# Expert rows fetched in two halves of 4 KB, and 24 sample slots ahead of the fence

## The chip, the cores and the metric

The kernel runs on one core of a Trainium2 chip. The metric is the device time of one execution, in microseconds. Three executions of the kernel before took 1599.02, 1606.98 and 1607.16 us. The core has five engines that work side by side and wait for one another by semaphores: PE (TensorE), DVE (VectorE), ACT (ScalarE), POOL (GpSimd) and SP (SyncE, which here only issues loads and stores). Sixteen DMA engines move the data between memory and the core for all of them.

## The reference

One decoder layer for 512 prompt tokens and 32 sample tokens (8 sequences of 4), all in float32. Retention heads and a convolution branch are mixed, added to the input and normalised; then every token goes through an expert layer, and is normalised again. The change lies in the expert layer:

```python
q = (xb @ w_query).reshape(PEER_BLOCK, PEER_HEADS, PEER_DQ)      # 8 heads
v1, i1 = lax.top_k(s1, PEER_TOPK)                                # 16 of 128 keys, twice
sv, ci = lax.top_k(cand, PEER_TOPK)                              # 16 of the 256 pairs
idx = e1 * N_KEYS + e2                                           # one of 16384 experts
gate = jax.nn.softmax(sv.astype(jnp.float32), axis=-1)
u = jnp.take(peer_u, idx, axis=0)
act = jax.nn.gelu(jnp.einsum('phkd,pd->phk', u, xb), approximate=False)
vv = jnp.take(peer_v, idx, axis=0)
return jnp.einsum('phk,phkd->pd', gate * act, vv)
```

Each token thus needs 8 x 16 = 128 experts, and each expert is a row u and a row v of 1024 numbers (4 KB each).

## The kernel before

The host puts u and v of an expert side by side in one row of 8 KB (the array uv) and lays out a second copy of u for matmuls (ut).

**Two ways through the expert layer.** The last 256 prompt tokens take the dense way: all 16384 experts are computed by matmuls, 128 keys at a time. A scoring stage (`scores_of`, L778) loads 0.5 MB of ut and makes 16 matmuls (L784); its result goes through a gelu on ACT. `build` (L855) makes the tokens' weights for each key from one-hot matrices (ACT L862 and L864, DVE L866 and L870, PE L875); `first_keys` (L888) multiplies them into the arrays Gb, Ga and Gc (DVE L899 and L901), `last_keys` (L907) makes Gd. A v stage (`v_stage`, L914) loads 0.5 MB of v rows and adds 8 matmuls to the sums in PSUM (L920). There are 128 scoring stages and 128 v stages; both take their loads from a pool of four buffers (`uvp`, L759), by SP's queue.

**The fetched way.** The other tokens, the first 256 of the prompt and the 32 samples, fetch only the experts that they need (`gather`, L567). A slot is one indirect transfer that POOL issues (L572): for each of 128 partitions the row of 8 KB that the index names, 1 MB in all. Then DVE multiplies the u half with the token and sums it (the dot, L575), ACT makes the gelu and multiplies it by the gate (L579, L580), and DVE adds v times that weight to the sum (the update, L585). Group 0 (`gather0`, tokens 0 to 127) has 128 slots, the samples s have 32 (each token on four partitions, with two heads on each), group b (tokens 128 to 255) has 128: 288 slots. The buffers are three in the pool `gp` (L99), and a fourth for every fourth slot, `gx` for the first 60 slots of group 0 and `gx2` for group b, which is opened behind the fence (L964). So samples that are fetched ahead of the fence have three buffers.

**Order of the work.** The program is written group by group, and a scheduler puts the instructions of each engine into one fixed order that it finds by its own estimate of the times. What the author adds are order constraints: the last instruction of `first_keys` is the fence (L963), and `gather` puts the dots of group b, and those of the samples from slot `FREE` on, behind it on DVE (L576, L577). `FREE` is 12 (L36): 12 sample slots may run ahead of the fence, 20 behind it. Behind the fence `run` (L597, L965) writes down the v stages, `last_keys` and the remaining 32 scoring stages (`phases`, L923), in turn with the rest of the slots (`fetched`, L944).

**What each step waits for.** A slot's transfer waits for the update that last read its buffer. The dot waits for the whole transfer. The update waits for ACT. The instructions of one engine run in their order, so a dot whose rows are late holds up everything behind it on DVE. The first multiply L899 frees the PSUM bank that the next matmuls of `build` write (two banks, `pdn`, L761). At the end, `finish` (L588) normalises the last group, and the two blocks of the dense way are normalised and stored (L966 to L971).

The indices come out of the top-k as floats; a cast on DVE writes them as integers into I0, Is and Ib (L685, L795).

Of the kernel before, what the change touches and what calls it, by code (L numbers as in the profile page):

```python
# [15 lines left out]
OP = mybir.AluOpType  # L16
# [3 lines left out]
D = 1024  # L20
# [12 lines left out]
TB = 8  # L33
KX = 60
UV = 4
FREE = 12  # L36
EG = (32, 20, 44, 32)
E0S = (0, 32, 52, 96)

# [54 lines left out]
def tile_step(ctx: ExitStack, tc: tile.TileContext, a, o):  # L94
    nc = tc.nc
    V, S, T, G = nc.vector, nc.scalar, nc.tensor, nc.gpsimd
# [17 lines left out]
    def mmps():  # L114
        turn[0] += 1
        return banks[turn[0] % len(banks)].tile([128, 512], F32, name="mm")
# [17 lines left out]
    def load_w(view, c0, places=(), after=None):  # L134

        ws = []
        for q in range(2):
            w = wp.tile([128, 8, 256], F32, name="w") if not places or places[q] is None else places[q]
            load = nc.sync.dma_start(w, view[c0 // 256 + q])
            if after is not None:  # L140
                behind(load, after)
            ws.append(w)
        return ws
# [21 lines left out]
    def behind(ins, other):  # L165
        tc.add_manual_dep(ins.ins, other.ins.name, mybir.DependencyInfo(
            mybir.DependencyClass.NoSync, mybir.DependencyReason.DATA), reason="order")

    def small(name, shape, dt=F32, bufs=2):
        return wk.tile(shape, dt, name=name, bufs=bufs)  # L170
# [24 lines left out]
    def project(w, m, xT, c0, n):  # L195
        p = mmps()
        for k in range(8):
            T.matmul(p[:, :n], w[m // 2][:, k, (m % 2) * 128:(m % 2 + 1) * 128], xT[:, k, c0:c0 + n],  # L198
                     start=(k == 0), stop=(k == 7))
        return p[:, :n]  # L200
# [366 lines left out]
    def gather(x1, idx, gate, acc, slots):  # L567

        for k in slots:
            spare = gx if x1 is x1_0 and k < KX else (gx2[0] if gx2 and len(slots) == 128 else None)  # L570
            t = (spare if spare is not None and k % 4 == 3 else gp).tile([128, 2 * D], F32, name="g")
            G.indirect_dma_start(out=t, out_offset=None, in_=a["uv"],  # L572
                                 in_offset=bass.IndirectOffsetOnAxis(ap=idx[:, k:k + 1], axis=0))
            act = gw.tile([128, 2], F32, name="act")
            dot = V.scalar_tensor_tensor(t[:, :D], t[:, :D], 1.0, x1, op0=OP.mult, op1=OP.mult, accum_out=act[:, 0:1])  # L575
            if fence and (len(slots) == 128 or k >= FREE):  # L576
                behind(dot, fence[0])  # L577
            wgt = gw.tile([128, 1], F32, name="wgt")
            S.activation(act[:, 1:2], act[:, 0:1], AF.Gelu)  # L579
            S.activation(wgt, act[:, 1:2], AF.Copy, scale=gate[:, k:k + 1])  # L580
            v = t[:, D:]
            if k == slots[0]:
                S.activation(acc, v, AF.Copy, scale=wgt)
            else:
                V.scalar_tensor_tensor(acc, v, wgt, acc, op0=OP.mult, op1=OP.add)  # L585
            yield
# [22 lines left out]
    E0 = per.tile([128, PH, TK], F32, name="E0")  # L609
    GT0 = per.tile([128, PH, TK], F32, name="GT0")  # L610
    I0 = per.tile([128, PH * TK], I32, name="I0")
    acc0 = per.tile([128, D], F32, name="acc")
    GSP = {"s": (32, 4), "b": (128, 1)}
    Eg, GTg, Ig = {}, {}, {}
# [46 lines left out]
    for q in range(2):  # L661
        c = slice(q * 512, (q + 1) * 512)
# [12 lines left out]
    for h0 in range(0, PH, 2):  # L675
        w = load_w(a["w_query"], h0 * 256)
        qq = small("qe", [128, 4, 128], bufs=1)
        for hs in ([h0], [h0 + 1]) if h0 == 0 else ([h0, h0 + 1],):
            for h in hs:
                for s in range(2):  # L680
                    m = (h - h0) * 2 + s
                    S.activation(qq[:, m], project(w, m, x1T0, 0, 128), AF.Copy)
            retrieve(lambda h, s: qq[:, (h - h0) * 2 + s], hs, 128, 1, E0, GT0, hs[0], led and (lambda ins: behind(ins, led[0])))
            ss = slice(hs[0] * TK, (hs[-1] + 1) * TK)
            c = V.tensor_copy(I0[:, ss], E0.rearrange("p h k -> p (h k)")[:, ss])  # L685
            led = led or [c]
    conv_s(yS)
    retain_s(qS, kS, vs[0], gS, last0)
# [2 lines left out]
    r = slice(NS, n)  # L691
# [98 lines left out]
    def topk_of(g, c0, which):  # L790
        w_, r_ = GSP[g]
        for h0 in which:
            retrieve(lambda h, s: qs[:, h * 2 + s, c0:c0 + w_], [h0] if r_ > 1 else [h0, h0 + 1], w_, r_, Eg[g], GTg[g], h0)
            ss = slice(h0 * TK, (h0 + (1 if r_ > 1 else 2)) * TK)
            V.tensor_copy(Ig[g][:, ss], Eg[g].rearrange("p h k -> p (h k)")[:, ss])  # L795

    for h0 in range(0, PH, 2):
        w = load_w(a["w_query"], h0 * 256)
# [6 lines left out]
    for g in range(2):  # L805
# [9 lines left out]
        p = mmps().rearrange("p (q t) -> p q t", q=4)  # L815
# [7 lines left out]
        for q in range(3):  # L823
            V.tensor_copy(gtT[:, q, cs], gr)
            if q < 2:
                V.tensor_sub(gr, gr, gtT[:, q, cs])
    topk_of("b", NS, range(0, PH, 2))
    topk_of("s", 0, range(2))
    for e in range(E0S[2], E0S[3]):
        S.activation(place(e), scores_of(e), AF.Gelu)  # L830
# [135 lines left out]
    for b in range(2):  # L966
        t = uvp.tile([128, D], F32, name="uv")
        layer_norm(t, 128, ln2[0], ln2[1], pB[b])
        for q in range(2):
            c = slice(q * 512, (q + 1) * 512)  # L970
# [47 lines left out]
```

## Time and profile before

| what | us |
|---|---|
| runs shown | 1599.02, 1606.98, 1607.16 |
| profiled execution | 1603.19 |
| its span, first to last instruction | 1601.4 |
| PE, DVE, ACT, POOL busy | 1494.5, 1225.3, 604.3, 374.1 |
| first slot of group 0 issued | 129.7 |
| sample slots issued, first and last | 776.5, 1065.3 |
| slots of group b issued, first and last | 992.6, 1567.4 |

The profile is of one execution. Busy times of engines overlap. In the windows, columns are: stretch and its length, busy us (and count) of PE, PEld (PE's weight loads), DVE, ACT and POOL, then the granted clock of PE, the mean busy share of the 16 DMA engines, and GB/s; asked for one line, only its engines have columns. In the timeline a row is start, duration, engine, line and operation, and in brackets how long the engine was idle ahead of it and what ended that. A line of the chain of waits is start, duration and what ran. In the table of transfers a row has minimum, median and maximum in ns, and the first and last start. The matmuls' ends are modelled, so the distance of starts says more than the busy share.

### The profile page before, as it was taken

How to read it: one execution, taken by the hardware profiler on the slowest of the kernel's cores; microseconds unless marked ns; L12 is line 12 of the kernel's file. 1: busy time of each engine (PE TensorE's matmuls, PEld its weight loads, DVE VectorE, ACT ScalarE, POOL GpSimd, SP SyncE). 2: the span in 40 equal slices, each digit the busy share in tenths (PEclk: the TensorE clock that was granted, in tenths of full speed). 3: DMA queues.
4: the chain of work that ended last, by engine and by line, in shares of the span. 5: the costliest groups of instructions: out<-in, count | busy, mean ns of one | idle time of the engine just before them, and what ended most of it. 6: DMA issues, size and time to landing. Idle time of an engine off the chain costs nothing.

```text
span 1601.4 us, 20802 instructions
## 1 busy us (share of the span) xinstructions
PE 1494.5 (93%) x7014; PEld 1010.1 (63%) x7014; DVE 1225.3 (77%) x3158; ACT 604.3 (38%) x1687; POOL 374.1 (23%) x335
## 2 busy tenths in 40 slices
PE   6899999996979999999999997999999999999996
PEld 6788556564756667788788875444566655543332
DVE  3939989989865999999852788566777777766666
ACT  2235542254222323333623888413994111111111
POOL 1001423444321222321120000122223222222221
PEclk9899999998989999999999997999999999999998
DMA  9458778997698669997794321998999999999995
GB/s 355 180 195 347 253 280 301 354 364 253 253 383 321 260 250 340 345 340 271 251 413 157 108 86 57 398 402 332 385 365 380 423 424 424 424 423 424 424 424 211
DMA packets 99543, 503.75 MB, mean 315 GB/s; under 512 B 10183, under 2 KB 21191, under 8 KB 56549
## 3 DMA queue, kind: packets, MB, share of 16 engines
q0 software_dynamic: 42240, 305.12, 48.7%
q1 hardware_dynamic: 50749, 189.96, 31.3%
q10 hardware_dynamic: 6448, 7.36, 1.5%
q8 instruction: 55, 0.90, 0.2%
q14 instruction: 51, 0.42, 0.1%
HBM read 497.03 MB, written 5.80 MB: 314 GB/s over the span
## 4 chain that ended last, share of the span: by engine, by line
PE 32%; DMA 28%; DVE 24%; issue 8%; ACT 4%; POOL 2%; SPq 0%; DVEq 0%; POOLq 0%; ACTq 0%
DMA g<-in_uv_dram,Ib 17%; PE pB L920 10%; PE sp L784 9%; PE mm L198 7%; DMA g<-in_uv_dram,I 7%; DVE acc L585 6%; DVE g L575 4%; POOL g L572 2%; ACT off L862 2%; PE mm L875 2%; PE mm L308 2%; DMA g<-in_w_in_dram 2%; DMA uv<-in_uv_dram 1%; DVE iu L504 1%; DVE score L505 1%
## 5 line engine op out<-in xcount | busy, mean ns | idle before, releaser
L784 PE MATMUL sp<-x1T,uv 128*128 128x256 f32 x2048 | 464.7, 384 | 15.4 <-ACT Ga L830 9.4
L784 PEld LDWEIGHTS sp<-x1T,uv 128*128 128x128 f32 x2048 | 385.5, 191 | 89.5 <-issue 23.2
L585 DVE SCALAR_TENSOR_TENSOR acc<-g,wgt,acc 128x1024 f32<-128x1024 f32 x285 | 365.0, 1281 | 99.3 <-ACT wgt L580 98.1
L572 POOL DMA_INDIRECT g<-in_uv_dram,I x128 | 181.9, 1421 | 435.1 <-DVE acc L585 222.6
L579 ACT ACTIVATE act<-act 128x1 f32<-128x1 f32 x288 | 57.9, 201 | 592.4 <-DVE g L575 592.0
L575 DVE SCALAR_TENSOR_TENSOR g<-g,x1g 128x1024 f32<-128x1024 f32 x160 | 195.3, 1224 | 94.2 <-DMA g<-in_uv_dram,Ib 63.1
L572 POOL DMA_INDIRECT g<-in_uv_dram,Ib x128 | 133.5, 1043 | 517.9 <-DVE acc L585 318.5
L575 DVE SCALAR_TENSOR_TENSOR g<-g,x 128x1024 f32<-128x1024 f32 x128 | 155.6, 1217 | 31.9 <-DMA g<-in_uv_dram,I 31.8
L198 PE MATMUL mm<-x1T,w 128*128 128x384 f32 (+1 forms) x512 | 176.1, 500 | 0.2 <-ACT score L524 0.2
L920 PE MATMUL pB<-uv,Ga 128*128 128x512 f32 x352 | 162.1, 604 | 1.1 <-DMA uv<-in_uv_dram 0.8
L862 ACT ACTIVATE off<-row,e1T 128x128 bf16<-128x128 bf16 x512 | 157.8, 388 | 1.5 <-PE mm L875 0.4
L198 PEld LDWEIGHTS mm<-x1T,w 128*128 128x128 f32 x512 | 96.6, 190 | 71.4 <-issue 37.9
L920 PE MATMUL pB<-uv,Gd 128*128 128x512 f32 x256 | 117.2, 601 | 2.1 <-DMA uv<-in_uv_dram 1.0
L920 PE MATMUL pB<-uv,Gb 128*128 128x512 f32 x256 | 115.4, 604 | 2.9 <-DMA uv<-in_uv_dram 2.5
L920 PEld LDWEIGHTS pB<-uv,Ga 128*128 128x128 f32 x352 | 63.7, 189 | 83.7 <-issue 63.1
L920 PEld LDWEIGHTS pB<-uv,Gd 128*128 128x128 f32 x256 | 46.1, 189 | 73.3 <-issue 48.2
L875 PEld LDWEIGHTS <-A 128*128 128x128 bf16 x1536 | 64.6, 100 | 36.6 <-issue 32.0
L920 PEld LDWEIGHTS pB<-uv,Gb 128*128 128x128 f32 x256 | 48.1, 193 | 59.6 <-issue 54.3
L875 PE MATMUL mm<-B,A 128*128 128x96 bf16 (+1 forms) x1536 | 68.4, 197 | 13.3 <-DVE Gc L901 12.4
L864 ACT ACTIVATE A<-off 128x1024 bf16<-128x1024 bf16 x64 | 67.4, 1053 | 28.1 <-PE mm L875 27.7
L870 DVE TENSOR_TENSOR B<-M,gtT 128x768 bf16<-128x768 bf16 (+1 forms) x192 | 69.8, 419 | 9.8 <-PE mm L875 9.6
L920 PE MATMUL pB<-uv,Gc 128*128 128x512 f32 x160 | 72.3, 599 | 0.0
(279 smaller groups left out, 1706.3 us busy)
## 6 DMA issues: line engine op xcount, KB each, us to landing
uv<-in_ut_dram SPq DMA_DIRECT2D x128, 512.0 KB
uv<-in_uv_dram SPq DMA_DIRECT2D x128, 512.0 KB
w<-in_w_in_dram SPq DMA_DIRECT2D x18, 1024.0 KB
w<-in_w_query_dram SPq DMA_DIRECT2D x16, 1024.0 KB
w<-in_w_out_dram SPq DMA_DIRECT2D x7, 1024.0 KB
g<-in_uv_dram,I POOLq DMA_INDIRECT x128, 7.9
keys<-in_state_retention_dram ACTq DMA_DIRECT2D x4, 512.0 KB
out_dram<-keys SPq DMA_DIRECT2D x4, 512.0 KB
```

The costliest lines, as they stand in the source:

```text
L198: T.matmul(p[:, :n], w[m // 2][:, k, (m % 2) * 128:(m % 2 + 1) * 128], xT[:, k, c0:c0 + n], start=(k == 0), stop=(k == 7))
L308: mm = T.matmul(p[:n, q * 256:(q + 1) * 256], xT[:, k, c0:c0 + n], w[q][:, k, :], start=(k == 0), stop=(k == 7))
L572: G.indirect_dma_start(out=t, out_offset=None, in_=a["uv"], in_offset=bass.IndirectOffsetOnAxis(ap=idx[:, k:k + 1], axis=0))
L575: dot = V.scalar_tensor_tensor(t[:, :D], t[:, :D], 1.0, x1, op0=OP.mult, op1=OP.mult, accum_out=act[:, 0:1])
L579: S.activation(act[:, 1:2], act[:, 0:1], AF.Gelu)
L585: V.scalar_tensor_tensor(acc, v, wgt, acc, op0=OP.mult, op1=OP.add)
L784: T.matmul(sp, u[:, k], x1T[:, k, NG2:], start=(k == 0), stop=(k == 7))
L862: S.activation(off[:, t], row, AF.Abs, bias=e1T[:, t1 + t:t1 + t + 1])
L864: S.activation(A, off, AF.Relu, bias=1.0, scale=-1.0)
L870: V.tensor_tensor(B[:, q], M, pairs_of(gtT[:, q], t1).to_broadcast([128, TB // 2, ne, 2]), op=OP.mult)
L875: T.matmul(pt[:, t % nt], A[:, t - t1], B[:, q, (t - t1) // 2, :, t % 2], start=(q == 0), stop=(q == 2))
L920: T.matmul(pB[b][q], W[:, b * 128:(b + 1) * 128], vt[:, q * 512:(q + 1) * 512], start=False, stop=(e == NK - 1), skip_group_check=True)
```

## The change

Each slot now comes by two indirect transfers into the two halves of the same buffer: first the u row, then the v row. For that the array uv is seen as rows of 4 KB, so the indices are doubled as they are written (a multiplication by 2 in place of the cast), and the second transfer starts 1024 numbers further on. The dot reads the first half, the update the second. `FREE` becomes 24: eight sample slots stay behind the fence instead of 20. The buffers, the rest of the order constraints and the dense way stay as they are; the scheduler orders the program anew.

```diff
-FREE = 12
+FREE = 24
...
-            G.indirect_dma_start(out=t, out_offset=None, in_=a["uv"],
-                                 in_offset=bass.IndirectOffsetOnAxis(ap=idx[:, k:k + 1], axis=0))
+            for half in range(2):
+                G.indirect_dma_start(out=t[:, half * D:(half + 1) * D], out_offset=None, in_=a["uv"].rearrange("r (q d) -> (r q) d", q=2),
+                                     in_offset=bass.IndirectOffsetOnAxis(ap=idx[:, k:k + 1], axis=0), element_offset=half * D)
...
-            c = V.tensor_copy(I0[:, ss], E0.rearrange("p h k -> p (h k)")[:, ss])
+            c = V.tensor_scalar(I0[:, ss], E0.rearrange("p h k -> p (h k)")[:, ss], 2.0, None, op0=OP.mult)
...
-            V.tensor_copy(Ig[g][:, ss], Eg[g].rearrange("p h k -> p (h k)")[:, ss])
+            V.tensor_scalar(Ig[g][:, ss], Eg[g].rearrange("p h k -> p (h k)")[:, ss], 2.0, None, op0=OP.mult)
```

## The prediction

> **What bounds the kernel now.** I read the page first: busy shares, then the row of transferred bytes by slice, then the two big queues.
>
> ```profile
> span 1601.4 us, 20802 instructions
> PE 1494.5 (93%) x7014; PEld 1010.1 (63%) x7014; DVE 1225.3 (77%) x3158; ACT 604.3 (38%) x1687; POOL 374.1 (23%) x335
> ...
> GB/s 355 180 195 347 253 280 301 354 364 253 253 383 321 260 250 340 345 340 271 251 413 157 108 86 57 398 402 332 385 365 380 423 424 424 424 423 424 424 424 211
> ...
> q0 software_dynamic: 42240, 305.12, 48.7%
> q1 hardware_dynamic: 50749, 189.96, 31.3%
> ```
>
> A slice is 1601.4/40 = 40 us. From the 32nd to the 39th, 1241 to 1561 us, the DMA engines move 423 to 424 GB/s without a break; from the 22nd to the 25th, 841 to 1001 us, they move 57 to 157. So one long stretch is full of transfers and the one ahead of it is nearly empty. q0 holds the fetched slots (288 of 128 rows of 8 KB, 302 of its 305 MB).
>
> Next, the windows of those two stretches, and from the chain and the timeline what TensorE does where it waits for nothing and where it does.
>
> ```profile
> 800.00:835.00 35.00, 35.00 (x164) 30.81 (x163) 21.87 (x27) 8.01 (x29) 7.84 (x9) 1.00 1.01 411
> 835.00:858.00 23.00, 23.00 (x108) 20.24 (x107) 0.00 (x0) 2.30 (x6) 0.59 (x1) 1.00 0.67 255
> 858.00:992.00 134.00, 118.30 (x1082) 101.57 (x1080) 101.59 (x381) 107.66 (x302) 0.00 (x0) 0.92 0.26 84
> ...
> 1400.00:1500.00 100.00, 98.62 (x223) 40.11 (x223) 68.26 (x83) 14.15 (x56) 25.14 (x27) 1.00 1.02 424
> ```
>
> ```profile
> 792.40 71.49 PE sp L784 x330
> ...
> 1035.97 44.73 PE pB L920 x104
> ```
>
> ```profile
> 1407.23 0.30 PEld L920 LDWEIGHTS pB<-uv,Ga 128*128 128x128 f32 x2 [0.35 <-DMA uv<-in_uv_dram]
> ...
> 1410.95 0.30 PEld L920 LDWEIGHTS pB<-uv,Ga 128*128 128x128 f32 x2 [0.85 <-DMA uv<-in_uv_dram]
> ...
> 1414.61 0.30 PEld L920 LDWEIGHTS pB<-uv,Ga 128*128 128x128 f32 x2 [0.79 <-DMA uv<-in_uv_dram]
> ```
>
> PE looks 98.6% busy at 1400 to 1500, but that share hides a wait. A v stage is 8 matmuls; unhindered, 104 of them took 44.73 us, 3.44 us a stage. In the full stretch stages start at 1407.23, 1410.95 and 1414.61: 3.69 us apart, the excess put down to the uv load. A scoring stage is 16 matmuls: 71.49/330 x 16 = 3.47 us. How many stages run, and how many slots (one acc update each):
>
> ```profile
> 992.00:1586.00 594.00, 188.82 (x147) 1.00 0.97 396
> 1400.00:1500.00 100.00, 34.29 (x27) 1.00 1.02 424
> ...
> 992.00:1586.00 594.00, 458.65 (x1008) 184.18 (x1008) 1.00 0.97 396
> 1400.00:1500.00 100.00, 94.98 (x207) 37.15 (x207) 1.00 1.02 424
> ...
> 992.00:1586.00 594.00, 117.64 (x512) 95.02 (x512) 1.00 0.97 396
> 1400.00:1500.00 100.00, 3.69 (x16) 2.96 (x16) 1.00 1.02 424
> ...
> 992.00:1586.00 594.00, 24.14 (x768) 23.66 (x768) 1.00 0.97 396
> ```
>
> (Windows of the lines L585, L920, L784 and L875; 992 is where the last multiply of first_keys frees what POOL waited 157 us for, 1586 where the last weights of PE are loaded.)
>
> ```profile
> 992.57 1.90 POOL L572 DMA_INDIRECT g<-in_uv_dram,Ib  x1 [156.99 <-DVE Gc L899]
> ...
> 1585.50 0.19 PEld L920 LDWEIGHTS pB<-uv,Gd 128*128 128x128 f32 x1 [0.24 <-issue]
> ```
>
> Behind the fence PE needs 126 x 3.44 + 32 x 3.47 + 24 = 569 us and takes 594: 25 us are lost. In 1400 to 1500 it does 25.9 + 1 stages, worth 92.6 us: 7.4 lost in 100; over the 320 us of the full stretch that is about 22. So the end is bounded by **TensorE, starved of its 0.5 MB loads by the fetches beside it**. The split shows how: 27 slots of 1.049 MB are 283 GB/s, 26.9 loads of 0.524 MB are 141. That is exactly 2 to 1, as is 8 KB against 4 KB: one slot row passes for each load row. The Trainium skill states such an order in DMA: Bandwidth & Descriptors, section Queues, rings and completion order: an engine takes turns between the queues that have work, a packet at a time. The rows agree, if a packet counts as one row here.
>
> **The change part by part.**
>
> *Half rows.* Bytes stay. If turns go by rows, 4 KB against 4 KB offers each queue up to half of 424, 212 GB/s. PE needs 0.524/3.44 us = 152, so it is no longer starved, and the slots get 424 - 152 = 272 GB/s, 3.86 us a slot instead of 3.71. **Gain at PE: of the 22 us I take 20**; bounds 0 (turns do not go by rows) and 25 (all that is lost).
>
> Does the slot stream then end last? Behind the fence it has 148 slots now and 136 afterwards. 12 fewer at 594/148 = 4.0 us are 48 us; the slower pace costs some 75 x 0.15 = 11. It ends 37 us earlier against the fence, PE 20 earlier: the stream has some 15 us in hand. What a half costs to issue is bounded by these rows:
>
> ```profile
> L572 POOL DMA_INDIRECT g<-in_uv_dram,I x128: 936/1071/7352, 129.7 to 738.1; - x128
> ...
> L572 POOL DMA_INDIRECT g<-in_uv_dram,Ib x128: 932/932/3545, 992.6 to 1567.4; - x128
> ```
>
> Two issues are 1.9 to 2.1 us of POOL, with a gap of 0.3 some 2.3: below 3.86, so POOL is no bound; the page has it at 23%, so about 40%. The dot needs only the u half, which lands ahead of the v half; the update comes 1.9 us after the dot starts (1.3 of dot, 0.6 for ScalarE), by when v is there. Both halves wait for the buffer's last update, so nothing is freed sooner. Row cost: q0 takes .487 x 16 x 1601.4/42240 = 295 ns for 7.2 KB, q1 .313 x 16 x 1601.4/50749 = 158 ns for 3.7 KB; a line through both gives 10.6 ns a row, so 128 more rows over 16 engines add 0.085 us a slot, some 8 us over 100 slots: inside the 15 in hand.
>
> *FREE 24.* These rows show where VectorE has room ahead of the fence:
>
> ```profile
> 799.20 1.23 DVE L575 SCALAR_TENSOR_TENSOR g<-g,x1g 128x1024 f32<-128x1024 f32 x1 [2.39 <-DMA g<-in_uv_dram,Is]
> ...
> 831.26 1.22 DVE L575 SCALAR_TENSOR_TENSOR g<-g,x1g 128x1024 f32<-128x1024 f32 x1 [0.84 <-DMA g<-in_uv_dram,Is]
> ...
> 833.09 1.28 DVE L585 SCALAR_TENSOR_TENSOR acc<-g,wgt,acc 128x1024 f32<-128x1024 f32 x1 [0.60 <-ACT wgt L580]
> 858.73 0.29 DVE L899 TENSOR_TENSOR Gb<-Gb,mm 128x128 f32<-128x128 f32 x1 [24.36 <-ACT Gb L835]
> ```
>
> Eight slots took 32.06 us, 4.0 each; then VectorE sat 24.4 us until ScalarE's Gb was ready. In the built order of the changed program 22 slots stand ahead of that first multiply instead of 12, and two behind it. Ten more at 4.0 reach 834.4 + 40 = 874. PE meanwhile has 176 scoring matmuls instead of 165 (two records each), until 792.4 + 352 x 0.2166 = 868.6, and then waits for a PSUM bank that the multiply frees: 5 us idle. Queued behind are the whole of first_keys, its v stages and the fence. The two slots inside cost VectorE 2 x (2.5 + 0.6) = 6 us, where it waits 31 us for PE in all:
>
> ```profile
> DVE Gb L899 <- PE mm L875: 31.2, 20, 4.4
> ```
>
> so they should be half hidden; but their updates wait for ScalarE in order, and I take 5. **Fence: +10**, bounds 0 (the earlier part gives VectorE a head start) and +33 (below).
>
> *The earlier part.* 128 slots of group 0 run beside projections and top-k. Loops get shorter by up to 1.9 us where the dot waited for the whole slot, which is this much:
>
> ```profile
> DVE g L575 <- DMA g<-in_uv_dram,I: 31.8, 27, 4.7
> ```
>
> Against that, the built order puts four more slots ahead of the second layer norm of the mix (4 x 2.5 = 10 us of VectorE, in a stretch where PE waits for that norm), and the norm's two small POOL steps stand behind one issue more:
>
> ```profile
> 416.73 2.96 POOL L572 DMA_INDIRECT g<-in_uv_dram,I  x1 [6.59 <-DVE lmv L448]
> 419.73 0.25 POOL L183 TENSOR_SCALAR lrs<-lmv 32x1 f32<-32x1 f32 x1
> ```
>
> Bounds: -15 (half of the 31.8) and +10; I take **-3**. The doubling of the indices replaces a cast of 0.2 us by one instruction of the same size: 0.
>
> *The end.* Now the slots' last layer norm mixes with the final one:
>
> ```profile
> 1581.60 1.28 DVE L585 SCALAR_TENSOR_TENSOR acc<-g,wgt,acc 128x1024 f32<-128x1024 f32 x1 [0.60 <-ACT wgt L580]
> ...
> 1588.18 1.22 DVE L454 TENSOR_TENSOR yt<-yt,lng 128x1024 f32<-128x1024 f32 x1
> ...
> 1589.99 1.22 DVE L455 TENSOR_TENSOR yt<-yt,lnb 128x1024 f32<-128x1024 f32 x1
> ```
>
> With the stream done earlier, those two leave it: **-2**.
>
> *Sum:* -20 + 10 - 3 - 2 = -15. The profiled execution took 1603.2 us (span 1601.4), 3.8 under the median of 1607.0. 1603.2 - 15 = **1588**.
>
> **The rivals.**
>
> *Fence late (slower).* If a slot of two issues ahead of the fence takes 4.6 us instead of 4.0 (three buffers, and issues that stretch to 1.7 as several of Ib do), VectorE is 7 us late after 12 slots and 46 more after 22: 887, PE idle for 19; and if the two slots inside wait 4.5 us for ScalarE each, as this one did,
>
> ```profile
> 488.27 1.28 DVE L585 SCALAR_TENSOR_TENSOR acc<-g,wgt,acc 128x1024 f32<-128x1024 f32 x1 [4.50 <-ACT wgt L580]
> ```
>
> they add 14: the fence is 33 late. -20 + 33 - 2 = +11, **1614**. It turns slower once the fence is over 22 late. For it: all engines are close there (118, 102, 108 of 134 us). Against: VectorE's 24.4 us and a stream that is DMA-bound (1.01), where u comes early.
>
> *The share stays 2 to 1.* Then starving lasts while slots run, 12 slots fewer: 12 x 0.27 = 3 us gained. -3 + 10 - 3 - 2 = +2, **1605**. For it: 800 to 835 is full too (1.01), and PE runs unhindered with three slot buffers, so it may be the slots in flight that count. Against: the exact 2 to 1.
>
> *Each transfer has a price of its own.* A slot's shortest way from issue to landing and the pause of the stream between the two groups:
>
> ```profile
> DMA to landing us min/median/max: 5.5/9.3/16.7
> ```
>
> ```profile
> 1076.15 1.28 DVE L585 SCALAR_TENSOR_TENSOR acc<-g,wgt,acc 128x1024 f32<-128x1024 f32 x1 [0.60 <-ACT wgt L580]
> ...
> 1092.08 1.21 DVE L575 SCALAR_TENSOR_TENSOR g<-g,x1g 128x1024 f32<-128x1024 f32 x1
> ```
>
> 1.049 MB at 424 GB/s are 2.5 us, so 3.0 of the 5.5 go with the transfer, not with its bytes. Four buffers turn once in 4 x 3.71 = 14.8 us. Were the 3.0 paid once more in each turn, with nothing to hide them, a slot would take 4.45, and 136 of them with the pause of 15 us 620: the stream would end last, at 992 + 10 - 3 + 620 = 1619 where the last stage ends at 1586 now: 1603 + 33 - 2 = **1634**. From 4.1 us a slot on it, not PE, ends last (999 + 136 x 4.1 + 15 = 1572, PE 1573). Against: in a full stretch the next slots are already queued while one lands. The same page of the Trainium skill, section Anatomy of one DMA — SWDGE (gpsimd) path, speaks against halving too: about 2.0 us for a transfer beside its bytes. By it the estimate for a slot is 16.8/4 = 4.2 us and the time about 1600; no run here shows that figure.
>
> *More.* No fence delay and the whole -15 ahead: -20 - 15 - 2 = -37, **1566**.
>
> **How the numbers follow.** Forecast 0.50, late fence 0.20, unchanged share 0.14, price per transfer 0.08, more 0.08. The forecast's own range is 1578 to 1598. The range 1572 to 1615 leaves out "more", the price per transfer and what of the late fence lies beyond its 1614. Half a per cent (8 us) is about what a measurement tells from no change. Faster: 0.45 of the forecast and 0.08, 0.53. Slower: 0.20 of the late fence, 0.04 of the unchanged share, 0.05 of the price, 0.29. Same: the rest, 0.18.
>
> **What would show it.** Right: v stages 3.44 us apart at 424 GB/s, with slots every 3.8 to 3.9 us; the last slot some 15 us ahead of PE; the first Gb multiply near 874 and the fence near 1002. Wrong: stages still 3.7 apart (share), VectorE waiting for landings to the very end with PE done (price), a PE gap over 15 us at 865 (fence), a mix layer norm later than now (earlier part).

## The result and the profile after

The changed kernel takes 1651.86 us (median of four runs, 1650.59 to 1656.75) where the kernel before takes 1607.07 (four runs, 1599.02 to 1610.07). The ratio is 1.0293, with a 95% interval of 1.0257 to 1.0329: **slower by 2.9%**. The forecast was 1588 in a range of 1572 to 1615. The profiled execution took 1656.75 us, the slowest of the four. In the new file each line from 574 on stands one lower than before (the update is L586, the scoring matmul L785, the v stage's L921, the first multiply L900).

The page of the changed kernel, in the rows that were read before:

```profile
span 1654.9 us, 21177 instructions
...
PE 1490.7 (90%) x7014; PEld 1022.4 (62%) x7014; DVE 1224.9 (74%) x3158; ACT 601.2 (36%) x1687; POOL 771.6 (47%) x623
...
GB/s 362 156 196 347 234 296 326 341 332 260 229 366 359 263 230 334 356 299 153 319 375 371 153 80 76 369 356 398 332 357 362 419 419 419 419 419 419 420 154 102
...
q0 software_dynamic: 83712, 305.14, 49.3%
q1 hardware_dynamic: 50749, 189.96, 30.6%
```

PE does the same work (1490.7 us, before 1494.5) in 53 us more, so it stands idle more. The full stretch is still there, at 419 GB/s instead of 424. The packets of q0 have nearly doubled (83712, before 42240) and its bytes have not. Where is PE idle? First the full stretch itself, as windows of L586 (updates), L921 (v stages) and L785 (scoring):

```profile
1400.00:1500.00 100.00, 33.44 (x26) 1.00 1.03 419
...
1400.00:1500.00 100.00, 68.94 (x159) 30.02 (x158) 1.00 1.03 419
...
1400.00:1500.00 100.00, 29.77 (x128) 23.66 (x128) 1.00 1.03 419
```

159/8 + 128/16 = 27.9 stages in 100 us, 3.59 each (before 3.72 over the same 100 us, forecast 3.44), and 26 slots, 3.85 each (forecast 3.86). So the share did move from the slots to PE, and the loss lies elsewhere. The SP queue's own timeline at the end:

```profile
1560.95 3.76 SPq L917 DMA_DIRECT2D uv<-in_uv_dram  x2
1590.84 0.34 SPq L596 DMA_DIRECT2D out_dram<-yt  x1
1591.27 40.28 SPq L917 DMA_DIRECT2D uv<-in_uv_dram  x13
```

The same queue in the kernel before:

```profile
1500.64 71.72 SPq L916 DMA_DIRECT2D uv<-in_uv_dram  x20
1591.24 0.34 SPq L595 DMA_DIRECT2D out_dram<-yt  x1
```

The chain of waits after, and PE's two longest new waits behind the fence:

```profile
1590.84 0.34 SPq L596
1591.27 5.64 DMA uv<-in_uv_dram
1597.05 47.89 PE pB L921 x104
```

```profile
PE pB L921 <- DMA uv<-in_uv_dram: 20.2, 2, 19.0
...
PE mm L876 <- ACT Gd L912: 12.0, 1, 12.0
```

The first new wait: SP issues in its fixed order, and the store of group b's result (L596) now stands **ahead of the last 13 v loads**. It waits for the last layer norm of the slots, until 1590.84, so the 13 loads wait too, and PE stands 19.0 us for the first of them. In the kernel before the same store stood behind every v load. The last row is another wait of 12.0 us on PE, taken up in e7. The rest lies ahead of the fence. The dense projections on PE (chain of waits, after), the windows of 400 to 500 us before and after, and PE's waits for the layer norms of the mix, two before and two after:

```profile
500.60 22.52 PE mm L198 x64
```

```profile
400.00:500.00 100.00, 85.24 (x378) 63.81 (x377) 66.04 (x92) 22.58 (x65) 30.39 (x28) 0.93 0.85 332
```

```profile
400.00:500.00 100.00, 59.40 (x294) 48.50 (x293) 68.18 (x98) 19.80 (x59) 61.75 (x53) 0.80 0.81 291
```

```profile
PE mm L486 <- DVE xr L455: 11.2, 1, 11.2
...
PE mm L486 <- DVE lrs L451: 3.5, 1, 3.5
```

```profile
PE mm L486 <- DVE lrs L451: 20.1, 1, 20.1
...
PE mm L486 <- DVE xr L455: 17.1, 1, 17.1
```

These projections started near 469.7 before. In that stretch PE drops from 85 to 59 us of 100, and waits 37 us (before 15) for the layer norms of the mix (L486 transposes what they give). From there everything is late, and the fence is no cause of its own:

```profile
898.34 0.29 DVE L900 TENSOR_TENSOR Gb<-Gb,mm 128x128 f32<-128x128 f32 x1 [1.75 <-ACT Gb L836]
...
1024.65 0.23 DVE L900 TENSOR_TENSOR Gc<-Gc,mm 128x80 f32<-128x80 f32 x1
```

The first Gb multiply comes 40 us later than before, but VectorE waits 1.75 us for ScalarE's gelu there, and that gelu (L836) had itself waited 2.65 us for PE's scoring: PE is as late as VectorE. The fence is at 1024.7 instead of 992.3.

### The profile page after: what moved, and what is told of

Its sections match the earlier page's. It is cut to its first block, busy times and chain, and to the rows that moved or that the text cites. A ratio compares the mean times of both kernels' runs of the same rounds, so it can differ in the third digit from the quotient of the medians.

```text
span 1654.9 us, 21177 instructions
## 1 busy us (share of the span) xinstructions
PE 1490.7 (90%) x7014; PEld 1022.4 (62%) x7014; DVE 1224.9 (74%) x3158; ACT 601.2 (36%) x1687; POOL 771.6 (47%) x623
## 3 DMA queue, kind: packets, MB, share of 16 engines
q0 software_dynamic: 83712, 305.14, 49.3%
## 4 chain that ended last, share of the span: by engine, by line
DMA 25%; DVE 21%; PE 19%; ACT 6%; POOL 6%; issue 6%; another core or an unknown queue 0%; DVEq 0%; POOLq 0%; SPq 0%; ACTq 0%
DMA g<-in_uv_dram,Ib 16%; PE sp L785 10%; DVE acc L586 6%; DMA g<-in_uv_dram,I 6%; POOL g L573 5%; PE pB L921 5%; DVE g L576 5%; DMA g<-in_uv_dram,Is 3%; ACT off L863 2%; PE mm L876 2%; PE mm L198 1%; ACT A L865 1%; DVE iu L504 1%; DVE score L505 1%; DVE B L871 1%
## 5 line engine op out<-in xcount | busy, mean ns | idle before, releaser
L785 PE MATMUL sp<-x1T,uv 128*128 128x256 f32 x2048 | 467.7, 385 | 16.1 <-ACT Ga L831 6.8
L573 POOL DMA_INDIRECT g<-in_uv_dram,Ib x256 | 327.4, 1279 | 299.9 <-PE mm L876 111.4
L573 POOL DMA_INDIRECT g<-in_uv_dram,I x256 | 338.4, 1322 | 270.4 <-DVE acc L586 96.7
L586 DVE SCALAR_TENSOR_TENSOR acc<-g,wgt,acc 128x1024 f32<-128x1024 f32 x285 | 365.4, 1282 | 132.6 <-ACT wgt L581 80.3
L785 PEld LDWEIGHTS sp<-x1T,uv 128*128 128x128 f32 x2048 | 387.6, 192 | 87.7 <-ACT W L884 14.7
L576 DVE SCALAR_TENSOR_TENSOR g<-g,x 128x1024 f32<-128x1024 f32 x128 | 155.6, 1216 | 42.4 <-DMA g<-in_uv_dram,I 41.7
L198 PE MATMUL mm<-x1T,w 128*128 128x384 f32 (+1 forms) x512 | 181.8, 510 | 5.2 <-ACT score L524 5.2
L921 PE MATMUL pB<-uv,Ga 128*128 128x512 f32 x352 | 155.9, 592 | 0.0
L921 PE MATMUL pB<-uv,Gd 128*128 128x512 f32 x256 | 113.3, 605 | 19.0 <-DMA uv<-in_uv_dram 19.0
L573 POOL DMA_INDIRECT g<-in_uv_dram,Is x64 | 81.0, 1266 | 99.1 <-DVE sv L506 35.9
L921 PE MATMUL pB<-uv,Gb 128*128 128x512 f32 x256 | 114.1, 600 | 1.6 <-DMA uv<-in_uv_dram 1.2
L921 PEld LDWEIGHTS pB<-uv,Ga 128*128 128x128 f32 x352 | 66.8, 190 | 71.8 <-issue 70.3
L921 PEld LDWEIGHTS pB<-uv,Gd 128*128 128x128 f32 x256 | 49.6, 194 | 82.5 <-issue 81.5
L876 PE MATMUL mm<-B,A 128*128 128x96 bf16 (+1 forms) x1536 | 68.7, 196 | 27.9 <-ACT Gd L912 12.0
L921 PEld LDWEIGHTS pB<-uv,Gb 128*128 128x128 f32 x256 | 47.8, 191 | 57.5 <-issue 54.8
L871 DVE TENSOR_TENSOR B<-M,gtT 128x768 bf16<-128x768 bf16 (+1 forms) x192 | 70.2, 419 | 17.8 <-PE mm L876 10.1
L921 PE MATMUL pB<-uv,Gc 128*128 128x512 f32 x160 | 76.6, 624 | 0.0
```

What stands on the lines that cost most here:

```text
L573: G.indirect_dma_start(out=t[:, half * D:(half + 1) * D], out_offset=None, in_=a["uv"].rearrange("r (q d) -> (r q) d", q=2), in_offset=bas ...
L785: T.matmul(sp, u[:, k], x1T[:, k, NG2:], start=(k == 0), stop=(k == 7))
L871: V.tensor_tensor(B[:, q], M, pairs_of(gtT[:, q], t1).to_broadcast([128, TB // 2, ne, 2]), op=OP.mult)
L876: T.matmul(pt[:, t % nt], A[:, t - t1], B[:, q, (t - t1) // 2, :, t % 2], start=(q == 0), stop=(q == 2))
L921: T.matmul(pB[b][q], W[:, b * 128:(b + 1) * 128], vt[:, q * 512:(q + 1) * 512], start=False, stop=(e == NK - 1), skip_group_check=True)
```

## The experiments

The theory after this reading: two orders that the scheduler chose anew make the loss, one in the front and one on SP's queue, and the halving itself gains what was forecast. The rivals: FREE 24 delays the fence, or each transfer has a price. "Order" means here the fixed order of each engine in the built program; where an experiment pins it, `behind(a, b)` puts instruction a after b. The medians of the kernel before in these series were 1601.7 to 1604.9 us; ratios go with the runs of before on the same chip. "Fence" is the start of the last multiply of `first_keys`, "PE done" the start of PE's last weight load, "slots done" the start of the last update, all in the profiled execution. That is one execution of each kernel, and its time can lie up to 10 us from the median (e5: 1597.9 against 1608.0), so a few us between two rows of these three columns tell little. Most of the differences are under 2%; a kernel is called faster or slower than the one before only where its interval leaves out 1.

| kernel | median us | ratio (95%) | fence | PE done | slots done |
|---|---|---|---|---|---|
| before | 1607.1 | 1 | 992.3 | 1585.5 | 1581.6 |
| changed | 1651.9 | 1.0293 (1.0257, 1.0329) | 1024.7 | 1643.9 | 1581.8 |
| e1 | 1627.1 | 1.0172 (1.0138, 1.0207) | 1011.2 | 1603.6 | 1601.1 |
| e2 | 1613.9 | 1.0086 (1.0054, 1.0119) | 989.3 | 1563.9 | 1584.8 |
| e3 | 1597.8 | 0.9966 (0.9945, 0.9987) | 989.9 | 1587.5 | 1531.5 |
| e4 | 1624.7 | 1.0152 (1.0124, 1.0181) | 1018.7 | 1609.5 | 1570.7 |
| e5 | 1608.0 | 1.0054 (1.0035, 1.0073) | 988.6 | 1579.2 | 1576.6 |
| e6 | 1667.1 | 1.0425 (1.0390, 1.0460) | 1050.1 | 1647.8 | 1645.3 |
| e7 | 1591.8 | 0.9938 (0.9918, 0.9958) | 987.5 | 1579.3 | 1545.0 |
| e8 | 1656.2 | 1.0341 (1.0311, 1.0371) | 992.8 | 1639.4 | 1565.4 |
| e9 | 1603.7 | 0.9986 (0.9965, 1.0006) | 994.4 | 1591.3 | 1546.7 |
| e10 | 1610.1 | 1.0028 (1.0009, 1.0046) | 990.0 | 1593.0 | 1587.0 |
| e11 | 1606.9 | 1.0017 (0.9999, 1.0034) | 988.9 | 1584.5 | 1581.4 |
| e12 | 1617.9 | 1.0073 (1.0049, 1.0097) | 992.3 | 1607.5 | 1578.9 |
| e13 | 1597.8 | 0.9977 (0.9954, 1.0000) | 983.4 | 1564.4 | 1570.5 |
| e14 | 1602.7 | 1.0001 (0.9980, 1.0021) | 986.1 | 1576.4 | 1576.6 |
| e15 | 1604.2 | 0.9996 (0.9969, 1.0022) | 1001.5 | 1587.8 | 1584.4 |
| e16 | 1637.8 | 1.0230 (1.0195, 1.0266) | 1013.3 | 1595.4 | 1616.4 |
| e17 | 1598.5 | 0.9968 (0.9949, 0.9987) | 989.4 | 1584.7 | 1530.5 |
| e18 | 1593.2 | 0.9949 (0.9931, 0.9967) | 989.4 | 1580.5 | 1545.9 |

### The parts one by one: e1, e2, e3, e4

e1 halves group 0 alone (and doubles only I0), FREE 12:

```diff
-            for half in range(2):
+            if x1 is x1_0:
+                for half in range(2):
...
+            else:
+                G.indirect_dma_start(out=t, out_offset=None, in_=a["uv"],
```

> Halves for the 128 slots of group 0 alone; the samples and group b come in 8 KB rows, FREE is 12. Theory (the front pays): the w_query projections of the dense way start near 500 us instead of 469.8, because POOL issues twice as often and because in the built order 67 instead of 64 slots stand ahead of the second layer norm of the mix and 87 instead of 80 ahead of the first top-k of those projections. The fence comes 25 to 31 us later than 992, and the end keeps its starving: 1603 + 28 = 1631 us (1624 to 1638). Rival A (FREE made the loss): nothing of it is here, 1603 within 5 us, projections before 475 us. Rival B (each transfer has a price, all along): some 10 us for 128 of 288 slots, 1613 us, with the later start spread over all of group 0 and no step at the mix norms.

1.0172: inside the theory's range. The projections started at 490.9, not 500, and the fence came 19 us late, not 25 to 31, with FREE as before and both other groups whole. So the front's loss belongs to group 0's halves.

e2 halves group b alone, FREE 12; the condition reads `len(slots) == 128 and x1 is not x1_0`.

> Halves for the 128 slots of group b alone, FREE 12: all up to the fence stands in the order of the kernel before. Theory (turns by rows): the fence stays at 992 within 3 us, the v stages of the full stretch start 3.45 to 3.58 us apart instead of 3.69, slots come every 3.8 to 3.9 us, no store stands ahead of a v load on SP's queue: 1603 - 16 = 1587 us (1582 to 1592). Rival (the share goes by slots in flight): stages stay 3.7 apart, 1603 within 4 us. Rival (price of each transfer): a slot takes over 4.1 us and the slot stream ends last, over 1603 us.

Half right. The windows of L928 (v stages) and L590 (updates) in e2, then its chain:

```profile
1400.00:1500.00 100.00, 100.00 (x234) 44.28 (x234) 1.00 1.03 419
...
1400.00:1500.00 100.00, 33.27 (x26) 1.00 1.03 419
```

```profile
1584.75 1.30 DVE acc L590
1586.07 1.29 DVE yt L597 x2
...
1600.23 0.60 DVEq L1022
```

234/8 = 29.25 stages in 100 us are 3.42 us each: PE is not starved at all, and is done 21.6 us earlier than before. But the kernel is slower, since now the **slots end last**: 148 of them at the slower pace are done at 1584.8, and their layer norm and the two final ones follow on VectorE. The profiled execution (1605.9) is the lowest of e2's runs. The rival's price is not what does it: a slot takes 3.85 us there, not over 4.1. The expectation had the gain at PE and forgot who is last after it.

e3 is the kernel before with `FREE = 24` and nothing else.

> FREE 24 alone: every slot in one transfer of 8 KB. 17 slots stand ahead of the first Gb multiply, not 12, and the store of group b's result stands ahead of the last 11 v loads on SP's queue. Theory: the fence moves by 0 to 8 us; behind it 12 slots fewer starve PE some 3 us less; the slots end near 1555 us, so SP is held by the store for little, 0 to 8 us: 1606 us (1600 to 1616). Rival (the fence makes the loss of the changed kernel): first Gb multiply near 895 instead of 858.7, 1603 + 33 = 1636 us.

1597.8, just under the expected range, and the fence at 989.9, no later than before. FREE 24 alone makes the kernel 0.3% faster (its interval ends at 0.9987). The slots are done at 1531.5, so the store ahead of 11 loads is issued at 1540.5 and holds nothing up.

e4 is the changed kernel with the last store moved:

```diff
-            nc.sync.dma_start(dst, t[p0:p1])
+            if n == 128 and x1 is not x1_0:
+                late.append((dst, t[p0:p1]))
...
     run((phases(), 1), (fetched(), 2))
+    for dst, t in late:
+        behind(nc.sync.dma_start(dst, t), loads[-1])
```

> The changed kernel, with the store of group b's result put behind the last v load on SP's queue; all else stands. Theory (head of SP's queue): PE loses its wait of 19 us near 1597 and the last stages follow 3.5 us apart: 1653 - 19 = 1634 us (1630 to 1639). Rival (the loads would have come late anyway, because slots still take their share, or the last layer norms on DVE end last): under 8 us gained, 1645 us or more.

1.0152 instead of 1.0293: 1.4 points or some 23 us go with the place of one store. That is more than the theory's range, and a little more than the 19 us of idle PE; in the two profiled executions the fence also differs by 6 us (the changed kernel's was the slowest of its four), which an edit at the end of the program hardly explains. That the store's place makes this loss is shown.

### Order or issue in the front: e5, e6

e5 is e1 with VectorE's old order in the front:

```diff
+        norms.append(V.bn_aggr(mv[:n], st[:n]))
...
+            if x1 is x1_0:
+                for at, ins in pins.items():
+                    if at <= k < at + 4:
+                        behind(dot, ins)
...
+    pins.update(zip((64, 65, 69, 73), norms[-4:]))
...
+    pins[80] = tops[16]
```

> e1 (halves in group 0 alone) with one thing more: dots 64, 65, 69, 73 of group 0 are put behind the four layer norms of the mix and dot 80 behind the first top-k of the dense projections, so that VectorE has the order of the kernel before there. e1 was 1627 us, 24 over before, and its projections started at 490.9 instead of 469.6 us. Theory O (the three to seven slots that the built order puts ahead of the norms make the loss): projections by 475 us, 1606 us. Theory L (a slot of two issues lands later, and the norms stand behind dots that wait): projections still at 485 us or later, 1618 us or more. Half and half, 1612 us, is what I hold likeliest.

1.0054 instead of 1.0172, nearer to theory O. First the projections on PE and the window of 400 to 500 in e1, then the same of e5:

```profile
490.94 22.78 PE L198 MATMUL mm<-x1T,w 128*128 128x416 f32 x64
```

```profile
400.00:500.00 100.00, 63.52 (x291) 48.81 (x291) 71.38 (x100) 22.00 (x65) 63.17 (x54) 0.81 0.86 304
```

```profile
470.07 23.44 PE L198 MATMUL mm<-x1T,w 128*128 128x416 f32 x64
```

```profile
400.00:500.00 100.00, 82.51 (x351) 61.08 (x350) 61.66 (x88) 21.87 (x60) 50.65 (x48) 0.90 0.86 313
```

With five slots fewer ahead of the last norm of the mix, the projections are back at 470 and the fence at 988.6. The updates of e1 between 420 and 500 us, as a window of that line:

```profile
420.00:500.00 80.00, 21.71 (x17) 0.77 0.88 318
```

17 in 80 us are 4.7 us a slot; five slots are 23 us, and the projections were 21 late. So two thirds of the front's loss, 1.2 of 1.7 points, is the built order. The 0.5% that is left is what halving group 0 costs in the old order. The profiled execution of e5, 10 us under its median, doesn't show where: its projections and its fence are as early as before.

e6 leaves the rows whole and adds a second, tiny transfer to each slot of group 0:

```diff
+            if x1 is x1_0:
+                G.indirect_dma_start(out=gw.tile([128, 16], F32, name="bit"), out_offset=None, in_=a["uv"],
+                                     in_offset=bass.IndirectOffsetOnAxis(ap=idx[:, k:k + 1], axis=0))
```

> The kernel before, in which each slot of group 0 is preceded by a second indirect transfer of 64 bytes for each partition into a scratch tile that nobody reads. POOL issues twice as often as before, the slots stay 8 KB rows in one transfer, 8 KB more in all move per slot, and the order of the slots and norms on VectorE is that of before within one slot. Theory (POOL's second issue of 0.93 to 1.9 us is what delays the slots and the norm's small steps on POOL): at least half of e1's 24 us, 1615 us or more, projections at 480 us or later. Rival (it is the 4 KB rows on their way that land late, or the built order): 1603 to 1608 us, projections by 473 us.

1.0425, far over what was to be told apart. POOL's timeline in e6 shows why:

```profile
448.18 0.95 POOL L573 DMA_INDIRECT bit<-in_uv_dram,I  x1 [0.30 <-issue]
449.44 0.95 POOL L573 DMA_INDIRECT bit<-in_uv_dram,I  x1 [0.30 <-issue]
450.69 1.13 POOL L573 DMA_INDIRECT bit<-in_uv_dram,I  x1 [0.30 <-issue]
452.13 0.94 POOL L575 DMA_INDIRECT g<-in_uv_dram,I  x1 [0.30 <-issue]
```

The tiny transfers did not go out in pairs with their slots. The scheduler bunched them, and a slot stands behind up to three of them, 1.25 us each. VectorE's order is that of the kernel before here (the norms stand behind 64, 65, 69 and 74 slots), so the loss shows that more issues on POOL are not free in the front even with hardly any bytes, but not what a pair of halves costs, so it does not decide between POOL and landing for e5's 0.5%.

### The share: e8

```diff
-        nc.sync.dma_start(vt, a["uv"][e * NK:(e + 1) * NK, D:])
+        for q in range(2):
+            nc.sync.dma_start(vt[:, q * 512:(q + 1) * 512], a["uv"][e * NK:(e + 1) * NK, D + q * 512:D + (q + 1) * 512])
```

> The kernel before, with each v load of 0.5 MB made as two loads of 2 KB rows on the same queue; slots stay 8 KB rows. Theory (queues take turns row by row): while slots run, the share is 4 to 1, a fifth of 424 GB/s is 85, so a v stage takes up to 6.2 us there instead of 3.69 and the slots come every 3.1 to 3.4 us; PE catches up only when the slots are done: 1650 us (1630 to 1690). Rival (the share goes by bytes or by transfers in flight): stages stay 3.7 apart, 1603 us within 8.

1656.2, as the theory of turns by rows said. PE's timeline in e8 (half stages of 4 matmuls):

```profile
1470.41 1.98 PE L921 MATMUL pB<-uv,Ga 128*128 128x512 f32 x4 [1.14 <-DMA uv<-in_uv_dram]
1473.50 1.98 PE L921 MATMUL pB<-uv,Ga 128*128 128x512 f32 x4 [1.10 <-DMA uv<-in_uv_dram]
1476.60 1.98 PE L921 MATMUL pB<-uv,Ga 128*128 128x512 f32 x4 [1.12 <-DMA uv<-in_uv_dram]
```

A half comes every 3.1 us, a stage every 6.2, which is a fifth of 424 GB/s. Together with e2 (4 KB against 4 KB, PE not starved) and the kernel before (8 KB against 4 KB, 2 to 1) this settles it: the queues share by rows. The trace of the kernel before has it in numbers of rows too: from 1400 to 1500 us 3448 rows of q0 (8 KB) and 3447 of q1 (4 KB) began. The rule of the Trainium skill in DMA: Bandwidth & Descriptors, section Queues, rings and completion order, agrees; how many rows go in one turn no run here shows.

### The parts put together: e7, e9

e7 is e2 with FREE 24 and e4's store.

> Halves for group b alone, FREE 24, and the store of group b's result behind the last v load. e2 ended with the slot stream (last update 1584.8) where PE was done at 1563.9; with 12 sample slots fewer behind the fence the stream ends some 12 x 3.9 = 47 us earlier, near 1540 to 1555, and PE ends last again at about 1564. Theory (the terms of the forecast hold where group 0 is left whole and SP is free): 1581 us (1575 to 1588). Rival (FREE 24 moves the fence later by 10 us or more): 1592 us or more.

1591.8, ratio 0.9938: faster, by half of what was expected, and outside the range. The fence is on time (987.5), and the slots end 34 us ahead of PE. But PE needs 1579.3 - 987.5 = 591.8 us behind the fence, not e2's 574.7, for the same 126 v stages and 32 scoring stages. PE's waits in e7, first from the fence to 1240 us, then in the full stretch, and ScalarE's timeline at the end of the first:

```profile
PE mm L886 <- ACT Gd L922: 10.1, 1, 10.1
```

```profile
PE sp L792 <- ACT W L894: 7.2, 11, 1.3
```

```profile
1110.74 0.20 ACT L584 ACTIVATE act<-act 128x1 f32<-128x1 f32 x1 [3.25 <-DVE g L580]
1110.97 0.29 ACT L585 ACTIVATE wgt<-act,GTb 128x1 f32<-128x1 f32 x1
1111.17 1.06 ACT L922 ACTIVATE Gd<-mm 128x512 f32<-128x512 f32 x2
```

PE's matmuls of `last_keys` wait 10.1 us for a PSUM bank that ScalarE's copy to Gd frees, and the scoring stages 7.2 us for ScalarE's gelu; the kernel before and e2 have no such wait for Gd, and with whole rows and FREE 24 it is 4.2 us (e3, e17). ScalarE runs in order, and in e7 the first Gd copy (L922) stands behind the weights (L585) of 27 slots past the fence, with FREE 12 behind 24; ScalarE idles 3.25 us for the last of these slots' dots and makes the copy right after it. These two waits make most of the 17 us between e7 and e2 (which has 4.3 us of the second).

e9 is the changed kernel whole, with the edits of e4 and e5.

> The whole change (halves in all 288 slots, FREE 24) with two orders mended: dots 64, 65, 69, 73 and 80 of group 0 stand behind the norms and the top-k as in the kernel before (e5), and the store of group b's result stands behind the last v load (e4). Theory (two orders that the scheduler chose made nearly all of the loss): projections by 475 us, fence near 990 us, 1600 us (1593 to 1608): e7's 1591.8 and the 6 us that e5 lost with halves in group 0. Rival (with all slots halved and FREE 24 the front is late for another reason): fence after 1005 us, 1615 us or more.

1603.7, ratio 0.9986: with the two orders mended, the change costs nothing that the interval shows. So the two of them make the whole 2.9%, as far as these intervals tell: the store 1.4 points (changed to e4), the front 1.7 (e4 to e9; projections at 477.0, fence at 994.4). It gains nothing either: PE needs 597 us behind the fence, with the same waits for Gd (8.9) and W (8.5).

### Moving the Gd copies: e10, e11, e12

```diff
-                S.activation(GW[3][:, :, ts], pt.rearrange("p t e -> p e t"), AF.Copy)
+                put = S.activation(GW[3][:, :, ts], pt.rearrange("p t e -> p e t"), AF.Copy)
+                at = 176 + 3 * (ts.start // 16) // 2
+                for ins in steps[at:at + 4]:
+                    behind(ins, put)
```

(`steps` holds the weight instructions of all slots; 176 in e10, 175 in e11 and e12.)

> e9 with one thing more: each ACT copy of a Gd part in last_keys is put ahead of three to seven of the slot weights that the built order has ahead of it (the first behind 176 slots instead of 179, the last behind 198 instead of 204). In e7 PE stood 10 us at 1101 to 1111 for the first of them, while ACT waited between slot weights for dots 3.8 us apart. Theory (in-order ACT: the copy stands behind slots that come slower than the scheduler thinks): that wait goes, 8 us less than e9, 1592 us (1585 to 1600). Rival (PE only waits elsewhere, for loads or for ACT): within 3 us of e9.

> e7 (halves in group b alone, FREE 24, store last) with each ACT copy of a Gd part put ahead of four to six more slot weights (first behind 175 slots instead of 179, last behind 197 instead of 203). Theory: PE's wait of 10 us at 1101 to 1111 goes, 8 us less than e7's 1591.8: 1584 us (1578 to 1589). Rival: PE waits elsewhere instead, within 3 us of e7.

> As e11 but with every slot in one transfer of 8 KB: FREE 24, store last, Gd copies ahead. Theory (turns by rows): PE is starved in the full stretch as in the kernel before, with stages 3.7 apart until the slots end, so it stands 10 to 14 us over e11: 1596 us (1590 to 1601), little under e3's 1597.8, whose wait for Gd was 4 us. Rival (the gain of e7 and e11 is FREE and order, not halving): within 4 us of e11.

All three missed: e10 is 0.4 points slower than e9, e11 0.8 slower than e7, e12 0.7 slower than the kernel before. The window of 1100 to 1150 in e7, then in e11:

```profile
1100.00:1150.00 50.00, 39.10 (x314) 20.27 (x313) 37.94 (x77) 38.47 (x113) 31.18 (x25) 0.90 0.98 371
```

```profile
1100.00:1150.00 50.00, 43.83 (x278) 21.65 (x277) 26.80 (x58) 27.70 (x80) 16.77 (x14) 0.93 0.85 302
```

PE gets 4.7 us back, and the slots now stand behind the copies: POOL issues 14 transfers instead of 25, the transfers fall from 371 to 302 GB/s, and the slots end at 1581.4 instead of 1545.0. In these orders ScalarE ties PE and the slot stream together: putting the copies earlier moved the wait from one to the other and did not remove it. What e12 does tell: beside e11, the same kernel with whole rows is 0.6 points slower, so in that order halving is worth some 9 us (its theory had 10 to 14), and their intervals do not meet.

### FREE between 12 and 24: e13 to e18

e13 and e14 are e7 with FREE 16 and 18, e15 is e9 with FREE 18, e16 the changed kernel with FREE 12.

> e7 with FREE 16 instead of 24. The first Gd copy stands behind 24 slots after the fence as with FREE 12 (27 in e7). Theory (FREE sets both ends): no wait of 10 us for Gd, PE behind the fence 576 to 582 us as in e2, done near 1568; the slots, 8 later than e7, end at 1545 + 8 x 3.9 = 1576 and then last: last update 1572 to 1578, 1593 us (1586 to 1598). Rival (halving itself makes PE wait in the stretch of last_keys): PE behind the fence 590 us, 1592 us or more with PE last.

> e7 with FREE 18. The first Gd copy stands behind 25 slots after the fence. Theory: a wait for it of 0 to 4 us, PE done near 1568 to 1572, the slots at 1545 + 6 x 3.9 = 1568: both end together, 1585 us (1580 to 1591), the lowest of these kernels. Rival (the wait for Gd comes in full with any FREE over 12): 1591 us, as e7.

> e9 (all slots halved, old order in front, store last) with FREE 18. Theory (FREE 24 takes the gain back): fence near 992, the wait for Gd 0 to 4 us, 1595 us (1588 to 1601), 6 to 10 less than e9. Rival: within 3 us of e9's 1603.7.

> The changed kernel with FREE back at 12; the scheduler's order is left alone, so the front stands as in e1 (67 and 87 slots ahead) and the store of group b behind all v loads. Theory: the front's 20 us at the fence (1011), PE done at 1011 + 576 = 1587, the slots as in e2 595 us behind the fence, at 1606, and last: 1622 us (1615 to 1630), 30 less than the changed kernel. Rival (FREE has no part in the loss): 1645 us or more.

e13 has the mechanism that was expected: no wait for Gd, PE done at 1564.4 (581 us behind the fence), slots last at 1570.5; its median is 5 us over the expectation but inside the range. e14 did not become the best: its slots took as long behind the fence (590 us) as e13's (587), though two fewer, and PE waited 6.0 us for Gd. Why its stream is slower is open. e15 shows no gain over e9, as its rival had it: PE needs 586 us behind the fence instead of 597, but in its profiled execution the fence is 7 us later, so a smaller FREE alone does not bring e9 to the forecast. e16 is 0.6 points faster than the changed kernel (their intervals just meet), not the 1.8 of the theory, and over its range: without the store's block it loses to the slots, which end at 1616.4, 21 us behind PE, as in e2.

e17 is e7 without halves (whole rows, FREE 24, store last), e18 is e7 again, on one chip:

> Whole rows of 8 KB, FREE 24, the store of group b's result behind the last v load: e7 without its halves. PE waited for no load behind that store in e3, so the store's place gives nothing here: 1598 us (1594 to 1602). Theory (halving group b is worth the 6 us between 597.6 and 591.8 behind the fence): 4 to 8 us over e18. Rival (the difference of e3 and e7 was the chip): within 2 us of e18.

> The kernel of e7 once more, beside e17 on one chip: 1592 us (1588 to 1596), 4 to 8 us under e17 by the theory, within 2 us of it by the rival.

0.9968 and 0.9949; the medians are 5.3 us apart as the theory has it, but the intervals overlap. That FREE 24 with whole rows is 0.3% faster than the kernel before is shown twice (e3 and e17), and that with halves in group b it is 0.5 to 0.6% faster is shown twice too (e7 and e18); that the halves add to FREE is likely, not shown by this pair. e7 is the fastest kernel here, some 3.4% under the changed one by the ratios.

## Why the prediction was wrong

**The gain at PE (-20): the mechanism was right, the gain went elsewhere.** Turns by rows are shown by e2 and e8, with 3.42 us a stage and 3.85 a slot against the forecast's 3.44 and 3.86; with FREE 12 PE needs 18.5 us less behind the fence (593.2 to 574.7). With FREE 24 little of the term is there: 592 us in e7, 591 in e4, 597 in e9, beside 595 to 598 with whole rows (e17, e3). The step that failed is "so it is no longer starved" as the end of the argument: PE then waits 10 and 7 us for ScalarE, in whose order the Gd copies and gelus stand behind the slots. Where the wait for Gd is absent, with FREE 16 (e13) and with FREE 12 and all slots halved (e16), PE needs 581 and 582 us. The prediction named no row of ScalarE behind the fence. (Its loss of 7.4 us in 100 makes 23.7 over 320 us, not 22; that changes nothing here.)

**The fence (+10): too dear.** e3, e7 and e17 have it at 987 to 990, before 992. There 17 slots, not 12, stand ahead of the first multiply, and they fit in the 24.4 us for which VectorE waited anyway. The 22 slots that the prediction counted stand there only in the changed kernel and e4, where the front is late. From the start of scoring (L785) to the fence these two take 502 us, e16 with 12 slots and the front as late 498, and the kernel before 500, so less than half of the 10 us is there. The fence of the changed kernel was 32 us late, close to the rival's 33, but not by that rival's mechanism: 19 of the 32 are there in e1, with FREE 12.

**The earlier part (-3, bounds -15 to +10): the step that failed first.** It measured 1.7 points, some 27 us of loss (e4 to e9; 19 at the fence in e1), where the worst bound was +10. The prediction read in the built order that more slots stand ahead of the norms, and priced them at 2.5 us of VectorE each. A slot there costs what the stream needs for it, 4.7 us in that stretch of e1, and the norm stands behind it in order while PE waits for the norm. The shorter loops that were to pay for it did not come: VectorE's dots wait 41.7 us for group 0's rows in the changed kernel, before 31.8. It also counted four more slots ahead of one norm and not on to the fourth norm (78 dots ahead, before 73) and the first top-k (87, before 80). Halving itself, in the old order, costs 0.5% (e5).

**SP's queue: not in the sum at all.** This is the second step that failed. The prediction compared orders on VectorE and POOL, and missed that a store which had stood behind every v load now stood ahead of 13. It was in the built order to be read. Measured: 1.4 points, some 23 us (e4).

**The v half: not always there.** The prediction held that the v half has landed when the update wants it. In group b the updates waited for it 35 times:

```profile
DVE acc L586 <- DMA g<-in_uv_dram,Ib: 32.5, 35, 1.4
```

In the full stretch the slots still came every 3.85 us, so the forecast's pace held.

**The end (-2): right.** From PE's last weight load to the last row of VectorE it is 6.4 us in the changed kernel (1643.9 to 1650.3), 9.2 before.

**The rivals.** "The share stays 2 to 1" fell with e2 and e8. "A price of its own" fell as priced: it needed over 4.1 us a slot, and 52 halves in 100 us are 1.92 us each, 3.85 a slot. The Trainium skill gives about 2.0 us for a transfer beside its bytes in DMA: Bandwidth & Descriptors, section Anatomy of one DMA — SWDGE (gpsimd) path; in the full stretch here that part is hidden. The rival's order of events, the slots ending last, came true in e2 and e16, by number of slots and not by price. "Fence late" had the size and the wrong cause.

Open: what e5's last 0.5% is (landing or POOL), why e14's slots are slow, and a way to free PE from ScalarE's order behind the fence.

## What to carry to other kernels

After any edit, read the built order on every queue, the one that only issues loads and stores too: a store that waits for the end of a slow stream must stand behind all loads that others wait for. An item put ahead of a waiting instruction costs the stream's pace at that place, not its own busy time. And when a starved engine is fed, ask at once who is last then, and which in-order engine between the two streams now makes one wait for the other.

## What was not expected of the hardware

Queues share the transfer engines by rows, to the digit: 8 KB against 4 KB gave 283 and 141 GB/s, 8 KB against 2 KB a v stage every 6.2 us while slots ran. Rows of 4 KB throughout move 419 GB/s where rows of 8 KB beside 4 KB moved 424. The issue of an indirect transfer of 64 bytes a row occupies POOL nearly as long as that of one of 8 KB a row: 1252 ns against 1312 in the mean of 128 each (POOL's groups in e6):

```profile
L575 POOL DMA_INDIRECT g<-in_uv_dram,I x128 | 168.0, 1312 | 267.2 <-DVE acc L588 124.8 <-DVE score L505 21.6 <-issue 14.4
L573 POOL DMA_INDIRECT bit<-in_uv_dram,I x128 | 160.2, 1252 | 78.5 <-issue 34.8 <-DVE vf L503 23.3 <-DMA bit<-in_uv_dram,I 20.3
```
